# Down projection of a two-layer hybrid encoder: tiles 3 to 18 as four block groups of four in one chain instead of eight, four plain and four

## The chip, the cores and the metric

The kernel runs on one core of one Trainium2 chip. The metric is device time in microseconds, the median of several executions of the program. All arithmetic is float32; a matmul is done in three passes over float32r high and low parts, so that one product of float32 matrices is three matmul instructions.

## What is computed

Two layers over 1040 frames (16 learned meta tokens and 1024 input frames) of width 1024. Each layer has an attention half (a gated-linear-attention head group beside a forgetting-attention head group, one output projection, residual add) and a gated feed-forward half. Only the last matrix product of the second half is touched here:

```
def conv_ffn(x, w_up, conv_w, conv_b, w_down):
    h = x @ w_up
    ...
    u, g = jnp.split(hc, 2, axis=-1)
    return (jax.nn.silu(g) * u) @ w_down

# in each layer
h = h + conv_ffn(rms_norm(h, ffn_norm[i]), w_up[i], conv_w[i], conv_b[i], w_down[i])
```

`w_down` is 2816 x 1024. The kernel holds it as 22 tiles of 128 rows (the gated tiles, numbered 0 to 21) by 8 column blocks of 128.

## The kernel before

Activations are kept transposed: 128 features on the partitions, frames along the row. The frames are worked on in two halves of 520 in layer 0 (0 to 519 and 520 to 1039) and, since the last layer drops the meta tokens, in two halves of 512 in layer 1. A half of 520 is two matmuls of 260 columns ("pieces"), a half of 512 is one matmul.

**The gated tiles.** The up-projection writes each of the 22 gated tiles `cv` to memory (`actd`, L1395). For the down projection they are read back as `st` (L1458, L1464) and split into high and low float32r parts, the high part by a cast on ScalarE (ACT), the low part by a subtraction on VectorE (DVE). `prepare` (L1447) does this. It is a generator: `pump` lets it go on by a step when enough buffers are free, and `complete` runs it until what is needed now exists.

**The groups.** `GROUPS` (L49) says how the sum over the tiles is cut:

- "n", tiles 0 to 2, plain: for each of 8 column blocks and each half the three tiles are multiplied; ACT copies the sum out of PSUM to `do`, and a DMA issued by GpSimd (POOL) adds it to the residual in memory (`hm`, L1688).
- "s", tiles 3 to 10, a block group: see below; the sums are added to `hm` by DMA (L1588).
- "r", tiles 11 to 14, plain: the residual is read from memory to `h` (L1659) ahead of it, and DVE adds the products out of PSUM onto it (L1684).
- "s", tiles 15 to 18, a block group; the residual is on chip now, so DVE adds the sums `du` and `dg` onto `h` (L1585).
- `LAST`, tiles 19 to 21, plain, follows in `down_last` beside the next stage's norm.

**A block group** (`down_blocks`, L1555) is one level of a Strassen-Winograd product. Two column blocks (a "pair" j, 4 pairs in all) by two halves of the group's tiles are a 2 x 2 block matrix of weights, and two halves of the tiles by two halves of the frames are a 2 x 2 block matrix of activations. Seven products p = 1 to 7 take the place of eight. Per group, seven activation operands `X[p]` are formed once, with four combinations on DVE (L1517) and seven splits (L368 on ACT, L369 on DVE). Per pair, seven weight operands are formed: up to four combinations on DVE (L1114), and for each a cast on ACT (`hi`, L1132) and a subtraction on DVE (`lo`, L1133). With eight tiles a weight operand is 128 x 512, with four it is 128 x 256, and a product is 24 or 12 matmuls in layer 0 (12 or 6 in layer 1). The order of the products is written out in `seq`; it lets the next pair's first product begin before the pair's last two. Out of PSUM, ACT copies (L1594) and DVE adds (L1593).

**What sets the order.** PE's instructions stand in the order of the program text. Those of the other engines are put in order by a scheduler, from when it expects each to be ready, except where the text pins one (`keep_in_program_order`). Each engine, and SyncE (SP) with the DMA loads it issues, then works strictly in its order. The weight operands are written `AHEAD` = 4 products ahead of the product that uses them, and a buffer that is being added to memory by DMA counts as free `LANDING` = 4 products later.

Of the kernel before, what the change touches and what calls it, by code (L numbers as in the profile page):

```python
# [23 lines left out]
T = META + SEQ  # L24
# [143 lines left out]
class Kern:  # L168
# [1278 lines left out]
    def prepare(self, halves, acts, X):  # L1447
# [37 lines left out]
        for kind, g0, ng in GROUPS + (("r",) + LAST,):  # L1485
            while len(ahead) < 2 and loads:
                yield size()
                fetch()
# [16 lines left out]
            for k0 in range(0, nk, 2):  # L1505
                m = min(2, nk - k0)

                def put(p, src):
# [4 lines left out]
                    self.split(h, l, src[:, :m, :W])  # L1513
                    X[g0][p].append(([hi, lo] if m == 2 else [hi], h, l))

                def tt(out, a, b, op):
                    nc.vector.tensor_tensor(out=out[:, :m, :W], in0=a[:, :m, :W], in1=b[:, :m, :W], op=op)  # L1517
                yield m
# [36 lines left out]
    def down_blocks(self, lyr, g0, ng, X, pp, fw, halves, after, hT):  # L1555
# [3 lines left out]
        nk, o0, W = ng // 2, halves[0], halves[2]  # L1559
# [8 lines left out]
        j, k = NP - 2, NP - 1  # L1568
        seq += [(j, 2), (j, 6), (j, 5), (k, 1), (j, 7), (k, 6), (j, 4), (j, 3), (k, 7), (k, 2), (k, 5), (k, 4), (k, 3)]
        raws, ops, st = {}, [], {}  # L1570
        wd = lambda m: self.wd[lyr, m][:, g0:g0 + ng, :]

        def ensure(i):
            while len(ops) < min(i + 1, len(seq)):
                j, p = seq[len(ops)]
                ops.append(self.block_operand(wd(2 * j), wd(2 * j + 1), nk, j, p, fw, raws, len(ops) % 2))
                if nk == 2 and p == 6 and j + 1 < NP:
                    self.block_raws(wd(2 * j + 2), wd(2 * j + 3), nk, j + 1, fw, raws)
# [3 lines left out]
        def hand_on(i, m, x):  # L1582
            if hT:
# [7 lines left out]
        def evacuate(i, j, p):  # L1591
# [17 lines left out]
            elif p == 4:  # L1609
                copy(q["g"][:, t0])  # L1610
                hand_on(i, 2 * j + 1, q["g"])
            elif p == 3:
                add(q["u"][:, t1], q["x"])
                hand_on(i, 2 * j, q["u"])
                del st[j]
        def run():
            self.among_blocks = True
            for i, (j, p) in enumerate(seq):
                ensure(i + AHEAD)
# [6 lines left out]
                ops[i] = None  # L1626
                for k in range(nk):
                    _, hi, lo = X[p][k // 2]
# [4 lines left out]
                while going and (going[0][0] <= i or i == len(seq) - 1):  # L1633
# [12 lines left out]
    def ffn_down(self, lyr, pp, fw, halves, acts, X, ids):  # L1646
# [9 lines left out]
        def load_residual():  # L1656
            for k in range(KD):
# [260 lines left out]
```

## Time and profile before

| | |
|---|---|
| time, median of 3 runs | 2490.31 us (2489.84 to 2492.92) |
| the profiled execution | 2491.14 us, of it the span of its instructions 2489.4 |
| granted TensorE clock, mean | 0.997 |
| TensorE busy | 2455.0 us, 18286 matmuls |
| VectorE busy | 1884.3 us |
| ScalarE busy | 1331.6 us |
| GpSimd busy | 386.7 us |
| DMA moved | 261.02 MB, mean 105 GB/s |
| down projection, layer 0: first plain matmul, first and last block product | 1007.4, 1041.8 and 1207 us |
| down projection, layer 1: first block product, last copy of one | 2279 and 2439 us |

In the profile, PE is TensorE's matmuls and PEld its weight loads, DVE is VectorE, ACT is ScalarE, POOL is GpSimd, and SP issues DMAs. A row names a line of the kernel, an engine, an operation and "out<-in" by the program's tile names. "idle before" is how long the engine stood idle just ahead of such rows, and behind the arrow is what ended it.

### The profile page before, as it was taken

What the parts mean: (1) busy time and instruction counts of PE and PEld (TensorE: products, weight loads), DVE (VectorE), ACT (ScalarE), POOL (GpSimd) and SP (SyncE); (2) the same over time, 40 slices, a digit from 0 to 9 for tenths busy, and PEclk for the clock granted to TensorE, in tenths of its full rate; (3) what the DMA queues carried; (4) which work ended last, traced back from release to release, by engine and by line L of the source; (5) the groups of instructions that cost most, each with busy time, mean ns of one, the idle gap of its engine ahead of it and who ended that gap; (6) DMA issues with size and microseconds to landing.
All of it is one profiled execution on the core that took longest, in us unless ns stands there. A gap on an engine that the chain in (4) does not pass through costs nothing.

```text
span 2489.4 us, 47411 instructions
## 1 busy us (share of the span) xinstructions
PE 2455.0 (99%) x18286; PEld 2361.6 (95%) x18286; DVE 1884.3 (76%) x3833; ACT 1331.6 (53%) x2889; POOL 386.7 (16%) x567
## 2 busy tenths in 40 slices
PE   9999999999999999999999999999999999999998
PEld 8999999999999999999999899999999999997886
DVE  8656776869988888865865666777699888887567
ACT  7346666636555555642543466666465555555433
POOL 2023333210000000100210334331100000001002
PEclk9999999999999999999999999999999999999999
DMA  3232134433322224763312222243433212247722
GB/s 134 67 90 68 47 97 125 129 119 111 108 82 81 88 67 143 196 171 120 111 52 77 75 76 73 70 142 108 146 81 115 90 64 90 76 160 178 211 69 87
DMA packets 122002, 261.02 MB, mean 105 GB/s; under 512 B 15264, under 2 KB 37024, under 8 KB 121776
## 3 DMA queue, kind: packets, MB, share of 16 engines
q1 hardware_dynamic: 97440, 182.81, 23.8%
q0 software_dynamic: 22464, 72.88, 10.3%
q8 instruction: 143, 2.34, 0.4%
q10 hardware_dynamic: 1872, 2.31, 0.3%
q14 instruction: 83, 0.68, 0.1%
HBM read 177.31 MB, written 67.85 MB: 98 GB/s over the span
## 4 chain that ended last, share of the span: by engine, by line
PE 67%; issue 16%; DVE 11%; ACT 4%; DMA 1%; POOL 0%; SPq 0%; DVEq 0%; POOLq 0%; ACTq 0%
PE mm L254 7%; PE mm L256 7%; PE mm L255 7%; PE up L254 5%; PE up L255 5%; PE up L256 5%; PE down L255 5%; PE down L256 5%; PE down L254 5%; PE av L752 3%; PE tr L726 2%; DVE S L693 1%; PE S L690 1%; PE wo L254 1%; PE wo L256 1%
## 5 line engine op out<-in xcount | busy, mean ns | idle before, releaser
L254 PE MATMUL up<-x,hi 128*128 128x260 f32 x2240 | 632.8, 283 | 0.1
L255 PE MATMUL up<-x,lo 128*128 128x260 f32 x2240 | 632.8, 283 | 0.0
L256 PE MATMUL up<-x,hi 128*128 128x260 f32 x2240 | 632.7, 282 | 0.1
L256 PEld LDWEIGHTS up<-x,hi 128*128 128x128 f32 x2240 | 422.0, 188 | 0.4 <-DVE x L1157 0.3
L254 PEld LDWEIGHTS up<-x,hi 128*128 128x128 f32 x2240 | 421.6, 188 | 0.5 <-DVE hg L1370 0.3
L255 PEld LDWEIGHTS up<-x,lo 128*128 128x128 f32 x2240 | 421.4, 188 | 0.1
L1132 ACT CAST hi<-raw 128x512 fp32r<-128x512 f32 (+1 forms) x490 | 265.5, 553 | 197.4 <-PE up L256 88.1
L254 PE MATMUL mm<-xh,hi 128*128 128x348 f32 (+4 forms) x1056 | 362.8, 344 | 0.0
L1133 DVE TENSOR_TENSOR lo<-raw,hi 128x512 fp32r<-128x512 f32 (+1 forms) x490 | 287.1, 600 | 84.1 <-ACT hi L1132 83.8
L256 PE MATMUL mm<-xl,hi 128*128 128x348 f32 (+4 forms) x1056 | 339.9, 322 | 0.0
L255 PE MATMUL mm<-xh,lo 128*128 128x348 f32 (+4 forms) x1056 | 339.4, 321 | 0.0
L254 PEld LDWEIGHTS mm<-xh,hi 128*128 128x128 f32 x1056 | 199.6, 189 | 5.2 <-issue 4.6
L255 PEld LDWEIGHTS mm<-xh,lo 128*128 128x128 f32 x1056 | 199.5, 189 | 0.7 <-issue 0.7
L256 PEld LDWEIGHTS mm<-xl,hi 128*128 128x128 f32 x1056 | 198.5, 188 | 0.4 <-issue 0.3
L1114 DVE TENSOR_TENSOR raw<-raw,raw 128x512 f32<-128x512 f32 (+1 forms) x230 | 147.2, 648 | 24.2 <-DMA raw<-in_wd_dram 21.9
L705 ACT ACTIVATE P<-S,m 116x460 f32<-116x460 f32 (+2 forms) x224 | 125.0, 562 | 71.0 <-DVE m L693 67.3
L255 PE MATMUL down<-x,lo 128*128 128x260 f32 (+1 forms) x504 | 161.2, 320 | 0.8 <-DVE lo L1133 0.8
L254 PE MATMUL down<-x,hi 128*128 128x260 f32 (+1 forms) x504 | 161.0, 319 | 0.0
L256 PE MATMUL down<-x,hi 128*128 128x260 f32 (+1 forms) x504 | 161.0, 319 | 0.0
L369 DVE TENSOR_TENSOR PT<-tr,PT 116x464 fp32r<-116x464 f32 (+3 forms) x240 | 122.9, 515 | 47.4 <-ACT PT L368 45.7
L221 ACT CAST hi<-raw 128x512 fp32r<-128x512 f32 (+2 forms) x152 | 87.3, 575 | 111.3 <-PE wo L256 37.5
L1395 POOL DMA_DIRECT2D actd<-cv x44 | 23.6, 537 | 745.5 <-DVE cv L1394 727.3
(310 smaller groups left out, 5996.1 us busy)
## 6 DMA issues: line engine op xcount, KB each, us to landing
raw<-in_wm_dram SPq DMA_DIRECT2D x330, 256.0 KB, 3.0
raw<-in_wd_dram SPq DMA_DIRECT2D x48, 256.0 KB, 4.6
actd<-cv POOLq DMA_DIRECT2D x22, 520.0 KB, 3.0
actd<-cv POOLq DMA_DIRECT2D x22, 512.0 KB, 3.1
cb<-cd SPq DMA_DIRECT2D x16, 520.0 KB, 4.0
hm<-h POOLq DMA_DIRECT2D x32, 260.0 KB, 2.8
kA<-kA SPq DMA_DIRECT2D x24, 260.0 KB, 4.0
kL<-kL SPq DMA_DIRECT2D x24, 260.0 KB, 4.5
```

Source lines behind the costliest of these rows:

```text
L221: nc.scalar.copy(hi[:, :n, :], raw[:, :n, :])
L254: nc.tensor.matmul(ps, wh, xh[:, c0:c0 + n], start=first, stop=False, skip_group_check=more)
L255: nc.tensor.matmul(ps, wl, xh[:, c0:c0 + n], start=False, stop=False, skip_group_check=more)
L256: nc.tensor.matmul(ps, wh, xl[:, c0:c0 + n], start=False, stop=last, skip_group_check=more)
L369: nc.vector.tensor_tensor(out=lo, in0=src, in1=hi.bitcast(F32), op=ALU.subtract)
L690: nc.tensor.matmul(S[:rows, :n], q["qA"][e][:, qs], q["kA"][e][:, c0:k1], start=True, stop=False)
L705: nc.scalar.activation(P[:rows, :n], S[:rows, :n], AF.Exp, scale=-1.0, bias=m[:rows, nch - 1:nch], accum_out=(den if nch == 1 else d3[:row ...
L726: nc.tensor.transpose(tr[:w, 3 - j, :rows], P[:rows, o:o + w], id_)
L752: nc.tensor.matmul(av[:, a:b], w.rearrange("p a b -> p (a b)"), x, start=(t == ts[0] and part == 0 and i == 0), stop=(t == last and i == 1))
L1114: nc.vector.tensor_tensor(out=q[out][:, :nk, :], in0=q[a][:, :nk, :], in1=q[b][:, :nk, :], op=op)
L1132: nc.scalar.copy(hi[:, :nk, :], src[:, :nk, :])
L1133: nc.vector.tensor_tensor(out=lo[:, :nk, :], in0=src[:, :nk, :], in1=hi[:, :nk, :].bitcast(F32), op=ALU.subtract)
```

## The change

`GROUPS` becomes five groups: "n" as before, and then four block groups of four tiles, 3 to 6, 7 to 10, 11 to 14 and 15 to 18. There is no "r" group left. The four run as one chain: `down_blocks` gets all of them, the pairs are numbered 0 to 15, and `seq` runs on from the last pair of a group to the first of the next as it does from pair to pair. The first three groups add to `hm` by DMA; the residual is read in the last group, six blocks after product 6 of its first pair and two after product 6 of its second, and the last group's sums are added on chip. The activation operands of a group are formed while the group ahead is multiplied; their casts and low parts are pinned to the program order there, and so are the residual's loads. `LANDING` is 8.

```
-GROUPS, LAST = (("n", 0, 3), ("s", 3, 8), ("r", 11, 4), ("s", 15, 4)), (19, 3)
+GROUPS, LAST = (("n", 0, 3), ("s", 3, 4), ("s", 7, 4), ("s", 11, 4), ("s", 15, 4)), (19, 3)
-LANDING = 4
+LANDING = 8
...
@@ prepare
-            while len(ahead) < 2 and loads:
+            while len(ahead) < (1 if kind == "s" and self.among_blocks else 2) and loads:
...
-                    self.split(h, l, src[:, :m, :W])
+                    hi_ = nc.scalar.copy(h, src[:, :m, :W])
+                    lo_ = nc.vector.tensor_tensor(out=l, in0=src[:, :m, :W], in1=h.bitcast(F32), op=ALU.subtract)
+                    if self.among_blocks:
+                        self.tc.keep_in_program_order(hi_)
+                        self.tc.keep_in_program_order(lo_)
...
+                for _ in range(2 if self.among_blocks else 0):
+                    yield 0
@@ down_blocks
-        NP = KD // 2
+        NP, N = KD // 2, KD // 2 * len(groups)
...
-        for j in range(1, NP - 2):
+        for j in range(1, N - 2):
             seq += [(j, 2), (j, 6), (j, 5), (j, 7), (j + 1, 1), (j, 4), (j, 3)]
...
-                if nk == 2 and p == 6 and j + 1 < NP:
-                    self.block_raws(wd(2 * j + 2), wd(2 * j + 3), nk, j + 1, fw, raws)
+                if p == 6 and j + 1 < N:
+                    self.block_raws(*wd(j + 1), nk, j + 1, fw, raws)
...
-            if hT:
+            m = 2 * (j % NP) + half
+            if j >= N - NP:
...
+                if p == 1 and j % NP == 0:
+                    complete(lambda: built(groups[j // NP]))
                 ensure(i + AHEAD)
...
-                if j == NP - 1:
-                    for held, _, _ in X.pop(p):
+                if j % NP == NP - 1:
+                    for held, _, _ in X[g0].pop(p):
                         s.put(*held)
-                    if len(ops) == len(seq):
-                        after()
-                    self.pump(1, 3)
-                elif j and p == 5:
+                if (j, p) == (N - NP, 6):
+                    load_residual(range(6))
+                if (j, p) == (N - NP + 1, 6):
+                    load_residual(range(6, KD))
+                if i % 2 and (j >= N - NP or not built(groups[j // NP + 1])):
                     self.pump(1, 4)
@@ ffn_down
-        def load_residual():
-            for k in range(KD):
+        def load_residual(which):
+            for k in which:
                 hT.append(s.get(F32, f"h{k}", first=ids))
-                nc.sync.dma_start(hT[k][:, o0:T], self.hm[k][:, o0:T])
+                self.tc.keep_in_program_order(nc.sync.dma_start(hT[k][:, o0:T], self.hm[k][:, o0:T]))
```

What moves on the engines, at two places. The first is VectorE in layer 0. Before, this is a piece of its queue in the only group of four, tiles 15 to 18, that carries the residual: `lo` are low parts of weight operands, `du` and `dg` sums of a pair, `h1` and `h0` the residual, `al` the low part of a tile of `LAST`.

```order
L1593 TENSOR_TENSOR dg_15286<-down_15257,dg_15286 128x520
L1133 TENSOR_TENSOR lo_15320<-raw2_15289,hi_15319 128x256
L1593 TENSOR_TENSOR du_15214<-down_15305,du_15214 128x520
L1133 TENSOR_TENSOR lo_15339<-raw2_15070,hi_15338 128x256
L1585 TENSOR_TENSOR h1_14685<-dg_15286,h1_14685 128x1040
L1593 TENSOR_TENSOR du_15214<-down_15257,du_15214 128x520
L1133 TENSOR_TENSOR lo_15357<-raw_15297,hi_15356 128x256
L1585 TENSOR_TENSOR h0_14683<-du_15214,h0_14683 128x1040
L1593 TENSOR_TENSOR du_15233<-down_15360,du_15233 128x520
L1133 TENSOR_TENSOR lo_15375<-raw2_15072,hi_15374 128x256
L1133 TENSOR_TENSOR lo_15393<-raw_15074,hi_15392 128x256
L1496 TENSOR_TENSOR al_15412<-st_14541,ah_15411 128x1040
```

Of the change, this is a piece of VectorE's queue in the second group, tiles 7 to 10, at its second pair. L1521 and L1514 are the lines that were L1517 and L369, L1603 was L1593; `x6`, `x5` and `x7` belong to the third group.

```order
L1521 TENSOR_TENSOR st_13408<-st_13417,t2_14523 128x1040
L1514 TENSOR_TENSOR x6_14526<-t2_14523,x6_14525 128x1040
L1133 TENSOR_TENSOR lo_14548<-raw_14425,hi_14547 128x256
L1133 TENSOR_TENSOR lo_14576<-raw2_14573,hi_14575 128x256
L1603 TENSOR_TENSOR dg_14563<-down_14534,dg_14563 128x520
L1521 TENSOR_TENSOR st_13414<-st_13414,t2_14523 128x1040
L1514 TENSOR_TENSOR x5_14568<-st_13408,x5_14567 128x1040
L1133 TENSOR_TENSOR lo_14603<-raw2_14571,hi_14602 128x256
L1133 TENSOR_TENSOR lo_14626<-raw2_14421,hi_14625 128x256
L1603 TENSOR_TENSOR du_14440<-down_14534,du_14440 128x520
L1514 TENSOR_TENSOR x7_14621<-st_13411,x7_14620 128x1040
```

In the place of residual additions and low parts of `LAST`, operations over a full row in both, stand combinations and low parts of the next group's activations, between the low parts of weights and the additions out of PSUM that are as wide as before.

The second place is SP's queue where the residual is read, layer 0. Before, the loads of `h` stand with weights of the plain group "r" (L212) and with tiles of `LAST` (L1458), ahead of most weights of the group 15 to 18 (L1099):

```order
L1659 DMA h5_14693<-hm5_106 128x1040
L1659 DMA h0_14683<-hm0_101 128x1040
L1458 DMA st_14822<-actd20_129 128x1040
L212 DMA raw_14882<-in_wd_dram 128x512
L1659 DMA h7_14697<-hm7_108 128x1040
L212 DMA raw_14940<-in_wd_dram 128x512
L1458 DMA st_15409<-actd21_130 128x1040
L1659 DMA h6_14695<-hm6_107 128x1040
L212 DMA raw_14998<-in_wd_dram 128x512
L1099 DMA raw_15056<-in_wd_dram 128x256
```

Of the change (L1674 was L1659), with the weights of the last group's first three pairs:

```order
L1674 DMA h0_15574<-hm0_101 128x1040
L1099 DMA raw2_15335<-in_wd_dram 128x256
L1099 DMA raw2_15337<-in_wd_dram 128x256
L1099 DMA raw_15477<-in_wd_dram 128x256
L1674 DMA h1_15576<-hm1_102 128x1040
L1458 DMA st_15604<-actd20_129 128x1040
L1458 DMA st_15656<-actd21_130 128x1040
L1099 DMA raw2_15479<-in_wd_dram 128x256
L1099 DMA raw2_15481<-in_wd_dram 128x256
L1099 DMA raw_15483<-in_wd_dram 128x256
L1674 DMA h2_15578<-hm2_103 128x1040
L1674 DMA h3_15580<-hm3_104 128x1040
```

The residual's loads moved in among the weight loads of the chain: `raw2_15335` and `raw2_15337` belong to the last group's first pair and now stand behind `h0`, and the weights of its second pair stand behind `h1` and two tiles of `LAST`.

More of the change, by code (lines that the diff above doesn't have):

```diff
@@ L1626, in run @@
                 ops[i] = None
+                g0 = groups[j // NP][0]
                 for k in range(nk):
-                    _, hi, lo = X[p][k // 2]
+                    _, hi, lo = X[g0][p][k // 2]
                     for c in range(pieces):
@@ L1670, in plain @@
                 complete(lambda: all(j in acts for j in range(g0, g0 + ng)))
-                if kind == "r" and not hT:
-                    load_residual()
             if kind == "n" and m == 0:
@@ L1693, in plain @@
                     s.put(*acts.pop(j))
-            if not (nxt and built(nxt)):
+            if not (nxt and built(nxt[0])):
                 self.pump(2)
@@ L1700, in ffn_down @@
             if kind == "s":
-                parts.append((g0, ng))
+                if not isinstance(parts[-1], tuple):
+                    parts.append(())
+                parts[-1] += ((g0, ng),)
                 continue
@@ L1717, in run @@
                 if not isinstance(part, list):
-                    complete(lambda: built(part))
                     blocks[1]()
@@ L1721, in run @@
                 if nxt:
-                    then = parts[i + 2] if i + 2 < len(parts) else []
-                    blocks = self.down_blocks(lyr, *nxt, X[nxt[0]], pp, fw, halves,
-                                              lambda t=then: t and len(ahead) < 2 and fetch(t), hT)
+                    blocks = self.down_blocks(lyr, nxt, X, pp, fw, halves, hT, load_residual, complete, built)
                 for k, t in enumerate(part):
@@ L1732, in run @@
                 ahead.clear()
-            if not hT:
-                load_residual()
             complete(lambda: all(j in acts for j in range(LAST[0], sum(LAST))))
```

20 lines of the change are left out of this document (11 added, 9 removed).

## Prediction

> **What bounds the kernel now.** I read the page's table of engines first, then stages of the down projection, then the waits inside them.
>
> ```profile
> PE 2455.0 (99%) x18286; PEld 2361.6 (95%) x18286; DVE 1884.3 (76%) x3833; ACT 1331.6 (53%) x2889; POOL 386.7 (16%) x567
> ```
>
> TensorE (PE) is busy in 99% of the span. Since matmuls overlap, I do not lean on that share but on how many start in a stretch. The next rows are two stretches inside the down projection, one for each layer, all of it between the first block product and the last: length, then busy us and (count) of PE, PEld, DVE, ACT and POOL, the granted clock, the DMA share and GB/s.
>
> ```profile
> 1042.00:1202.00 160.00, 160.00 (x1337) 160.00 (x1337) 94.59 (x148) 61.30 (x109) 7.66 (x9) 1.00 0.51 141
> 2282.00:2438.00 156.00, 156.00 (x675) 126.48 (x674) 96.00 (x151) 59.65 (x107) 6.83 (x8) 1.00 0.50 140
> ```
>
> A matmul of 260 columns takes 160/1337 = 0.1197 us in layer 0, and one of 512 columns 156/675 = 0.2311 us in layer 1, at a granted clock of 1.00 and with no idle PE. So this part ends when PE ends, and its length is the number of matmuls. Only the run-up in layer 1 has holes:
>
> ```profile
> 2250.00:2260.00 10.00, 9.91 (x43) 7.78 (x42) 10.00 (x11) 9.02 (x14) 2.70 (x4) 1.00 0.55 105
> 2260.00:2270.00 10.00, 9.81 (x43) 7.64 (x42) 7.94 (x9) 6.17 (x9) 1.31 (x2) 1.00 0.93 222
> 2270.00:2280.00 10.00, 9.18 (x40) 7.19 (x39) 10.00 (x13) 8.91 (x16) 3.19 (x4) 1.00 1.05 194
> ```
> ```profile
> PE down L255 <- DVE lo L1133: 0.8, 1, 0.8
> PE down L254 <- ACT do L1686: 0.2, 1, 0.2
> ```
>
> PE loses 0.09 + 0.19 + 0.82 = 1.1 us there. The second fence (who waited for whom between 2240 and 2290: us, times, longest) puts 0.8 us of it on the first weight operand of the block group, which VectorE (DVE) forms behind the activation operands of eight tiles.
>
> **The change, part by part.** *Matmuls.* The two groups of four out of tiles 3 to 10 multiply as often as the group of eight did: 4 pairs x 7 products x 2 x 2 x 2 x 3 = 672 in layer 0. Tiles 11 to 14 were plain, 8 x 2 x 4 x 2 x 3 = 384; as a block group they need 4 x 7 x 2 x 2 x 3 = 336. That is 48 fewer in layer 0, and, with one piece for two, 24 fewer in layer 1: 48 x 0.1197 + 24 x 0.2311 = 5.74 + 5.55 = **11.3 us less on PE**, on the path.
>
> [...]
>
> *DVE.* What it needs per block group of four: 28 subtractions for the low parts of weights, 16 combinations of weights (both 256 wide), 12 additions out of PSUM, and 11 operations over a full row (four combinations and seven low parts of the next group's activations; in the last group eight residual additions and three low parts). Rows by shape (count | busy us, mean ns), layer 0 and then layer 1:
>
> ```profile
> L1133 DVE TENSOR_TENSOR lo<-raw,hi 128x256 fp32r<-128x256 f32 x28 | 11.0, 417 | 2.4 <-ACT hi L1132 2.4
> L1593 DVE TENSOR_TENSOR du<-down,du 128x520 f32<-128x520 f32 x15 | 10.4, 692 | 3.6 <-PE down L256 3.6
> ...
> L369 DVE TENSOR_TENSOR x<-st,x 128x1040 fp32r<-128x1040 f32 x6 | 7.3, 1235 | 3.9 <-DMA hm<-du 3.9
> L1114 DVE TENSOR_TENSOR raw<-raw,raw 128x256 f32<-128x256 f32 x16 | 6.3, 420 | 1.9 <-DMA raw<-in_wd_dram 1.8
> ```
> ```profile
> L1593 DVE TENSOR_TENSOR du<-down,du 128x512 f32<-128x512 f32 x16 | 11.0, 684 | 4.3 <-PE down L256 4.3
> L1496 DVE TENSOR_TENSOR al<-st,ah 128x1024 fp32r<-128x1024 f32 x7 | 8.5, 1221 | 4.1 <-ACT ah L1495 4.1
> ```
>
> By durations a group costs 28 x 0.417 + 16 x 0.420 + 12 x 0.692 + 11 x 1.235 = 40.3 us in layer 0, and 40.1 in layer 1. PE needs 336 x 0.1197 = 40.2 and 168 x 0.2311 = 38.8. That would be too much, but rows in a queue that is not waiting start before the one ahead has ended. This is DVE in the last group of layer 0 (start, duration or span of xN):
>
> ```profile
> 1182.64 0.69 DVE L1593 TENSOR_TENSOR du<-down,du 128x520 f32<-128x520 f32 x1
> 1183.25 0.75 DVE L1133 TENSOR_TENSOR lo<-raw,hi 128x256 fp32r<-128x256 f32 x2
> 1183.92 1.23 DVE L1496 TENSOR_TENSOR al<-st,ah 128x1040 fp32r<-128x1040 f32 x1
> 1185.07 0.75 DVE L1133 TENSOR_TENSOR lo<-raw,hi 128x256 fp32r<-128x256 f32 x2
> 1185.74 1.09 DVE L1114 TENSOR_TENSOR raw<-raw,raw 128x256 f32<-128x256 f32 x3
> 1186.75 0.69 DVE L1593 TENSOR_TENSOR dg<-down,dg 128x520 f32<-128x520 f32 x1
> ```
>
> From start to start an addition takes 0.61 us, a 256-wide row 0.335, a full row 1.15. So a group takes 44 x 0.335 + 12 x 0.61 + 11 x 1.15 = 34.7 us: 86% of PE's time in layer 0 and 89% in layer 1. The nearest stage is the last group of before, which has the same 28, 16, 12 and 11, though some of them are done ahead of it:
>
> ```profile
> 1168.00:1208.00 40.00, 40.00 (x336) 40.00 (x335) 30.66 (x55) 21.55 (x46) 0.00 (x0) 1.00 0.17 47
> 2400.00:2440.00 40.00, 40.00 (x174) 32.39 (x173) 30.87 (x56) 22.07 (x48) 0.00 (x0) 1.00 0.16 47
> ```
>
> DVE is busy for 31 of 40 us and PE has no hole. Four such groups in a row, each some 4 us fuller, still leave DVE 4.1 to 5.5 us of slack per group. I cost DVE's extra rows at nothing; PE's 40 us hide them. At full durations, with no cover, they cost 4 x 0.1 + 4 x 1.3 = 5.6 us.
>
> *ACT* casts and copies, and one row of POOL that is used below:
>
> ```profile
> L1132 ACT CAST hi<-raw 128x256 fp32r<-128x256 f32 x28 | 11.2, 409 | 24.1 <-PE down L256 20.7 <-DMA raw<-in_wd_dram 2.8 <-ACT hi L1132 0.6
> L1594 ACT COPY du<-down 128x520 f32<-128x520 f32 x16 | 9.5, 593 | 17.1 <-PE down L256 14.3 <-DMA hm<-do 2.7
> ...
> L368 ACT CAST x<-st 128x1040 fp32r<-128x1040 f32 x6 | 6.4, 1063 | 10.7 <-DMA hm<-dg 6.5 <-DVE st L1517 2.7 <-DVE al L1496 1.5
> ```
> ```profile
> L1588 POOL DMA_DIRECT2D hm<-du x4 | 3.4, 847 | 8.9 <-DVE du L1593 5.4 <-DVE raw L1114 3.4
> ```
>
> 28 x 0.409 + 16 x 0.593 + 7 x 1.063 = 28.4 of 40 us, hidden. Landing 8 instead of 4 keeps the same time, 8 x 1.44 = 11.5 us against 4 x 2.87: a product is now 12 matmuls, 1.44 us, and was 24. The new pins hold casts and low parts of activations in the written order, so that one that waits for its load has copies out of PSUM (ACT) or additions (DVE) behind it, and PE waits for those; the loads are issued a group ahead, so I cost the pins at nothing.
>
> *DMA.* Two more groups add into memory, 16 transfers of 520 KB per layer. Queues in layer 0 between 1041 and 1120 us (packets, MB, share of 16 engines):
>
> ```profile
> q1 hardware_dynamic: 4488, 9.36, 35.1%
> q0 software_dynamic: 1282, 4.73, 34.8%
> ...
> hm<-du POOLq DMA_DIRECT2D x3, 520.0 KB, 7.0
> ```
>
> 4.73 MB are 8.9 such transfers in 0.348 x 79 = 27.5 us, 3.1 each, so 16 cost 50 us of the engines. The part had a share of 0.51 over 160 us, 82 us; it becomes 132 in 154, 0.85. That fits, and an addition lands in 7.0 us, inside the 11.5. Their issue is 16 more rows on POOL of 0.85 us, 14 us in a queue that the first stretch shows busy for 8 of 160. The residual's eight loads, on SP's queue, now stand among the weights of the last group instead of ahead of plain tiles; the lead of one pair (7 x 1.44 = 10 us) covers them. I cost DMA at nothing, with this bound: the longest waits of DVE for weights in the two parts were these (the idle time before the row, and what ended it, in brackets):
>
> ```profile
> 1055.93 1.42 DVE L1114 TENSOR_TENSOR raw<-raw,raw 128x512 f32<-128x512 f32 x2 [9.07 <-DMA raw<-in_wd_dram]
> ```
> ```profile
> 2292.37 1.42 DVE L1114 TENSOR_TENSOR raw<-raw,raw 128x512 f32<-128x512 f32 x2 [8.43 <-DMA raw<-in_wd_dram]
> ```
>
> 9.1 and 8.4 us, both ended some 13 us into the group of eight. They cost PE nothing, because four operands formed ahead were 11.5 us of work. Four operands are now 5.7 us in layer 0 and 5.5 in layer 1, so such a wait would cost 3.4 + 2.9 = 6.3 us.
>
> *Run-up.* Half of the activation operands that DVE formed before the first block product are now due 40 us later, so the 0.8 us hole in layer 1 should close (between 0 and 1.1). *New small waits:* between nothing and the rivals below; the nearest row is what PE waited in this part of before, 0.8 + 0.2, so I take 1.0.
>
> **Sum:** -11.3 - 0.8 + 1.0 = -11.1 us. From the profiled execution, 2491.14 us (span 2489.4 and 1.7 around it), that gives 2480.0; it ran 0.8 us above the median of 2490.31, so I predict **2479.2**.
>
> **Rivals.** *DVE becomes the bound.* If rows cost their full durations, PE waits 5.6 us: 2484.8. For it: 86 to 89% leaves little when DVE also waits for casts. Against it: the start-to-start rows above.
>
> [...]
>
> *Weights late at the head of the chain.* The 9.1 and 8.4 us waits come again, with half the cover: 2479.2 + 6.3 = 2485.5. For it: the additions of the plain group crowd the DMA engines there as before. Against it: a pair's weights are half as many bytes.
>
> *Slower.* With a DMA share of 0.85 the same wait comes at the head of every group, where the next group's activations, or the residual, go through SP ahead of weights while additions are in flight: four times per layer, 4 x 6.3 = 25 us, 2504. It decides from the fourth wait on (12 us), and beyond 0.2% slower from the sixth.
>
> *No gain.* If a group's activations are not formed in time, PE stands at three borders per layer, and a third of the 13 us of forming each set would eat the gain: about 2490.
>
> **How the numbers follow.** Forecast 0.55, DVE bound 0.13, late weights 0.17, slower 0.10, no gain 0.05. A measurement of this kernel can tell about 0.2%, 5 us, from no change, so the line lies at 2485.3. Faster: 0.55, most of the DVE case (0.10) and half of the late weights (0.09), 0.74; slower 0.10; the rest 0.16. The range runs from all gains without new waits (2490.31 - 11.3 - 1.1 = 2477.9, a little under it) to 1.5 above the third case: 2477.5 to 2487, which holds 0.85.
>
> **What would show it.** Right: 72 fewer matmuls, down-projection stretches with PE at its full count up to the last block product, each about 5.6 us shorter; DVE near 9 tenths there with gaps that PE does not share; the hole at 2275 gone. Wrong: PE rows "down" that wait for low parts of weights (DVE bound, if DVE is then without idle; late weights, if DVE itself waits for raw), for activations, or SP waiting on additions into memory ahead of weight loads.

## The result, and the profile after

The changed kernel takes 2528.05 us, median of 4 runs (2522.28 to 2532.76), against 2490.08 (2489.84 to 2492.92) before: a ratio of 1.0143, 95% interval 1.0131 to 1.0155. It is 38 us slower where 11 us faster was forecast. The profiled execution took 2526.35 us, its span is 2524.6 and its mean granted clock 0.990 (0.997 before).

The row of engines from the page, and the two stretches inside the chain, one for each layer (length, then PE, PEld, DVE, ACT, POOL, granted clock, DMA share, GB/s):

```profile
PE 2459.2 (97%) x18214; PEld 2360.2 (93%) x18214; DVE 1936.4 (77%) x4023; ACT 1387.9 (55%) x3055; POOL 415.2 (16%) x599
```
```profile
1040.00:1200.00 160.00, 144.71 (x1159) 143.46 (x1160) 113.77 (x219) 87.23 (x177) 23.87 (x28) 0.95 0.80 183
2280.00:2440.00 160.00, 147.22 (x598) 115.87 (x597) 113.77 (x220) 84.31 (x174) 24.67 (x29) 0.95 0.82 187
```

The 72 matmuls are gone. But at the rates of before, 1159 matmuls need 138.7 us and 598 need 138.2: 43 of these 320 us are lost. PE stands idle for 15.3 + 12.8 = 28 of them; most of the other 15 are the clock, 0.95 where it was 1.00. Who waits for whom on PE, from the plain group to the end of the chain (us, times, longest), first layer 0, then layer 1:

```profile
PE down L254 <- DVE dg L1603: 10.4, 4, 5.6
PE down L254 <- DVE du L1603: 4.7, 2, 3.5
PE down L254 <- ACT do L1699: 3.3, 1, 3.3
```
```profile
PE down L254 <- DVE dg L1603: 7.3, 5, 3.6
PE down L254 <- DVE du L1603: 4.2, 2, 3.1
PE down L254 <- ACT do L1699: 2.3, 1, 2.3
```

15 waits, 32.2 us: 13 of them, 26.6 us, for an addition out of PSUM on DVE (`dg`, `du`, L1603), two, 5.6 us, for a copy out of PSUM on ACT (`do`). The span grew by 35.2 us although 11.3 us of matmuls left it, so 46.5 went. 32.2 are the idle time. The trace's record of the granted clock has the rest: in the two chains the clock falls to 0.50 seven times, for 34 us together, and PE works in 28 of these, which costs it 14.0 us. Why was the addition late? The longest wait, 5.6 us, begins at 1057.03 and ends at 1062.64. DVE ahead of it (start, duration, in brackets the idle time before and what ended it):

```profile
1049.37 0.42 DVE L1133 TENSOR_TENSOR lo<-raw,hi 128x256 fp32r<-128x256 f32 x1 [0.95 <-ACT hi L1132]
1056.96 0.88 DVE L1114 TENSOR_TENSOR raw<-raw,raw 128x256 f32<-128x256 f32 x2 [7.17 <-DMA raw<-in_wd_dram]
1057.77 1.23 DVE L1514 TENSOR_TENSOR x<-st,x 128x1040 fp32r<-128x1040 f32 x1
1058.92 0.42 DVE L1133 TENSOR_TENSOR lo<-raw,hi 128x256 fp32r<-128x256 f32 x1
1059.25 1.24 DVE L1521 TENSOR_TENSOR st<-st,t 128x1040 f32<-128x1040 f32 x1
1060.41 1.23 DVE L1514 TENSOR_TENSOR x<-st,x 128x1040 fp32r<-128x1040 f32 x1
1061.56 0.42 DVE L1133 TENSOR_TENSOR lo<-raw,hi 128x256 fp32r<-128x256 f32 x1
1061.89 0.69 DVE L1603 TENSOR_TENSOR dg<-down,dg 128x520 f32<-128x520 f32 x1
```

DVE stood 7.17 us at a combination of weights whose load had not landed. The addition that PE waited for is behind it in DVE's queue. PE's wait begins only after the load has landed: DVE then has two combinations, two low parts and three rows of 1040 columns for the next group's activations to do, 4.9 us, before it comes to the addition. So the rows of the change lengthen a wait that a late load began. In layer 0 DVE lost 27.1 us in 7 such waits, in layer 1 30.8 in 10:

```profile
DVE raw L1114 <- DMA raw<-in_wd_dram: 27.1, 7, 7.2
```
```profile
DVE raw L1114 <- DMA raw<-in_wd_dram: 30.8, 10, 6.9
```

ACT is held up in the same way: ahead of the copies of `do` that PE waits for until 1040.23 it stands at the cast of a late weight.

```profile
1038.26 1.02 ACT L1132 CAST hi<-raw 128x256 fp32r<-128x256 f32 x3 [7.46 <-DMA raw<-in_wd_dram]
```

And SP, which issues those loads in order (L1099), itself stood 112 us of layer 0's chain until weight buffers had been read. Before, it stood 66 us there, so waiting for buffers is not new by itself. After:

```profile
SPq L1099 <- DVE lo L1133: 68.7, 28, 10.5
SPq L1099 <- DVE raw L1114: 43.1, 17, 11.6
```

### The profile page after: what moved, and what is told of

The parts are those of the page before. It is cut to its first block, busy times and chain, and to the rows that moved or that the text cites. A ratio compares the mean times of both kernels' runs of the same rounds, so it can differ in the third digit from the quotient of the medians.

```text
span 2524.6 us, 47927 instructions
## 1 busy us (share of the span) xinstructions
PE 2459.2 (97%) x18214; PEld 2360.2 (93%) x18214; DVE 1936.4 (77%) x4023; ACT 1387.9 (55%) x3055; POOL 415.2 (16%) x599
## 5 line engine op out<-in xcount | busy, mean ns | idle before, releaser
L1132 ACT CAST hi<-raw 128x256 fp32r<-128x256 f32 (+1 forms) x602 | 296.8, 506 | 209.9 <-PE up L256 88.1
L1133 DVE TENSOR_TENSOR lo<-raw,hi 128x256 fp32r<-128x256 f32 (+1 forms) x602 | 317.5, 543 | 83.8 <-ACT hi L1132 82.9
L254 PE MATMUL down<-x,hi 128*128 128x260 f32 (+1 forms) x672 | 221.5, 330 | 26.7 <-DVE dg L1603 17.7
L255 PE MATMUL down<-x,lo 128*128 128x260 f32 (+1 forms) x672 | 219.5, 327 | 0.0
L256 PE MATMUL down<-x,hi 128*128 128x260 f32 (+1 forms) x672 | 219.1, 326 | 0.0
L1114 DVE TENSOR_TENSOR raw<-raw,raw 128x512 f32<-128x512 f32 (+1 forms) x294 | 165.0, 571 | 61.9 <-DMA raw<-in_wd_dram 59.2
L254 PEld LDWEIGHTS down<-x,hi 128*128 128x128 f32 x672 | 130.5, 194 | 42.2 <-DVE dg L1603 21.0
L369 DVE TENSOR_TENSOR PT<-tr,PT 116x464 fp32r<-116x464 f32 (+3 forms) x240 | 123.0, 515 | 47.3 <-ACT PT L368 45.7
```

Of the source, the lines that this page charges most:

```text
L254: nc.tensor.matmul(ps, wh, xh[:, c0:c0 + n], start=first, stop=False, skip_group_check=more)
L255: nc.tensor.matmul(ps, wl, xh[:, c0:c0 + n], start=False, stop=False, skip_group_check=more)
L256: nc.tensor.matmul(ps, wh, xl[:, c0:c0 + n], start=False, stop=last, skip_group_check=more)
L369: nc.vector.tensor_tensor(out=lo, in0=src, in1=hi.bitcast(F32), op=ALU.subtract)
L1114: nc.vector.tensor_tensor(out=q[out][:, :nk, :], in0=q[a][:, :nk, :], in1=q[b][:, :nk, :], op=op)
L1132: nc.scalar.copy(hi[:, :nk, :], src[:, :nk, :])
```

## The experiments

The theory after this: weights land too late, DVE waits for them with additions out of PSUM behind it, PE waits for the PSUM buffer (`down`) that they read, and the granted clock falls behind each wait. The rivals: DVE or ACT has too much to do; DMA engines full of additions into memory; the residual's burst. "After" below is the changed kernel. The kernel before was run again beside each round of runs, so a ratio is not exactly the quotient with 2490.08.

| run | us, median | ratio to before | 95% interval |
|---|---|---|---|
| e1_packed | 2508.57 | 1.0069 | 1.0054 to 1.0084 |
| e2_packed_lead2 | 2501.72 | 1.0044 | 1.0028 to 1.0061 |
| e3_no_adds | 2501.19 | 1.0037 | 1.0025 to 1.0048 |
| e4_spread | 2525.14 | 1.0129 | 1.0106 to 1.0151 |
| e5_ahead5 | 2532.75 | 1.0154 | 1.0137 to 1.0171 |
| e6_lead2_spread | 2501.25 | 1.0034 | 1.0023 to 1.0046 |
| e7_lead2_spread_head | 2509.97 | 1.0068 | 1.0053 to 1.0083 |
| e8_before_stall | 2511.68 | 1.0077 | 1.0062 to 1.0092 |
| e9_paced | 2505.85 | 1.0063 | 1.0046 to 1.0079 |
| e10_paced_only | 2535.32 | 1.0175 | 1.0160 to 1.0190 |
| e11_split_only | 2523.80 | 1.0127 | 1.0106 to 1.0147 |
| e12_no_pins | 2581.86 | 1.0365 | 1.0349 to 1.0380 |
| e13_no_weight_loads | 2480.80 | 0.9957 | 0.9942 to 0.9972 |
| e14_act_queue | 2523.05 | 1.0120 | 1.0100 to 1.0141 |
| e15_act_queue_late | 2511.01 | 1.0082 | 1.0059 to 1.0105 |
| e16_pieces | 2500.34 | 1.0040 | 1.0026 to 1.0054 |
| e17_spread_forming | 2511.97 | 1.0085 | 1.0071 to 1.0099 |
| e18_lead3_late | 2486.64 | 0.9981 | 0.9972 to 0.9990 |

### Are late weights the whole cause?

After, with the chain's weights filled in place of loaded:

```
# block_raws, nk == 2
-    nc.sync.dma_start(q[name][:, :nk, :], src[:, k0:k0 + nk, :])
+    nc.gpsimd.memset(q[name][:, :nk, :], 0.01)
```

> The kernel after with the chain's weights not loaded: GpSimd fills their buffers with 0.01 (so the four groups multiply by constants), everything else is the same, the same casts, low parts, combinations, additions into memory, activation and residual loads, pins. Theory: late weights are the whole cause; with weights always there PE has no wait over 1 us in the chains and the forecast of the prediction comes true, 2477 to 2483. If DVE or ACT is too full, or activations or residual come late, waits of PE stay without weights too: over 2487.

2480.80 us: the forecast, to 1.6 us. Two stretches inside the chain of this kernel:

```profile
1050.00:1200.00 150.00, 150.00 (x1255) 150.00 (x1255) 128.17 (x242) 93.06 (x192) 36.40 (x77) 1.00 0.70 150
2290.00:2440.00 150.00, 149.89 (x645) 120.64 (x645) 129.66 (x246) 90.16 (x188) 35.02 (x74) 1.00 0.67 146
```

PE has no hole beside a DVE that is busy for 128 and 130 of 150 us with all rows of the change. DVE and ACT are not the bound; one wait of 2.3 us is left in layer 0, for weights of the plain group, and one of 0.5 in layer 1. The run takes more away, though, than the lateness of weights: their load on the DMA engines too (share 0.70 where after has 0.80), and their place in SP's queue, so that activations and the residual go out earlier.

One part of the change alone, the group of eight as two groups of four:

```
-("s", 3, 4), ("s", 7, 4), ("s", 11, 4), ("s", 15, 4)
+("s", 3, 4), ("s", 7, 4), ("r", 11, 4), ("s", 15, 4)   # r: plain, residual read ahead of it
```

> One part of the change alone: tiles 3 to 10 as two block groups of four in one chain, tiles 11 to 14 plain as before, the last four a chain of their own, the residual loaded ahead of the plain tiles as before. No matmul is saved; there are 8 more additions into memory per layer. Theory of late weights (products of half the time, loads the same number of products ahead, that land as late as before): the stalls of the first two groups come as in the kernel after, 17.8 us of idle PE and half as much lost clock: 2508 to 2520. If the third group or the residual inside the chain is what makes the chain late: 2490 to 2496.

2523.80 us, by its ratio 32 us over before; 2508 to 2520 had been expected, and it lies above that. The split, which saves no matmul, brings the loss (1.0127 of 1.0143). The rest of the change saves all 72 matmuls, 11 us, and the total is no better for it, so it must lose at least as much again. In the split's profiled execution (2517.12 us, the fastest of four) PE waits 21.5 us in the plain group and the two groups of four behind it, none in the last group. The first row is layer 0's, the others are layer 1's:

```profile
PE down L254 <- DVE du L1603: 7.3, 1, 7.3
```
```profile
PE down L254 <- DVE dg L1603: 6.0, 3, 4.4
PE down L254 <- ACT dg L1604: 5.9, 1, 5.9
```

What did the split halve? Not the lead. In a group of eight, before, a pair's weights are asked for only with its first operand, four products of 2.87 us, 11.5 us, ahead of the combination that DVE waits at. The changed kernel asks for them three products earlier: the combination is seven products of 1.44 us, 10 us, behind. So "loads the same number of products ahead", as the expectation has it, is not how the text stands for a group of eight. What halved is the time that the weight buffers hold. They are the same buffers in both, for two pairs at most: 2 x 7 x 2.87 = 40 us of PE's work in a group of eight, 20 us in a group of four, where each is half empty. SP can't issue a load until a buffer has been read (the 112 us above), and what a load needs to land did not halve. Loads of weights inside the chain of layer 0 (KB each, median us from issue to landing), before and after:

```profile
raw<-in_wd_dram SPq DMA_DIRECT2D x15, 256.0 KB, 5.3
```
```profile
raw<-in_wd_dram SPq DMA_DIRECT2D x57, 128.0 KB, 5.9
```

### Do operands formed ahead cover a late weight?

```
-AHEAD = 4
+AHEAD = 5
```

> The kernel after with five operands formed ahead in place of four. If operands formed ahead are the cover against late weights, as the prediction had it, one more covers 1.44 us (1.39 in layer 1) of each of the 12 or so stalls of PE, and some 15 us of idle PE and 6 to 8 us of lost clock go: about 2505. If the additions out of PSUM that stand behind the waiting DVE instruction stop PE, and not a missing operand, the order on DVE shifts by one operand and nothing is gained: 2522 to 2534.

2532.75: nothing gained. An operand more in hand is no cover, because the wait holds the additions out of PSUM too, and PE stops where it needs their PSUM buffer: in the trace of this run as in after's, all of PE's waits in the chains (36 us) are for additions and copies out of PSUM, none for an operand (`hi`, `lo`).

### Buffers, lead and additions

In a group of four each weight buffer was half empty. Two matrices share one, and then the loads come a pair earlier as well:

```
# block_raws, nk == 2: one tile for A11 and A12, one for A21 and A22, one for S1 and S2
# e2, down_blocks, in place of "if p == 6 and j + 1 < N: self.block_raws(j + 1)"
+ if p == 6:
+     for a in (j + 1, j + 2): ... self.block_raws(*wd(a), nk, a, fw, raws)
```

> In the block groups the two weight halves of a matrix share one buffer, and the two sums S1 and S2 share one, so the same memory holds 4 and 3.5 pairs of weights where it held 2 and 1.75; each load is still issued at the same product of the pair ahead. If the weight loads stand on the queue because their buffers are not free (SP waits 112 us for readers of weight buffers in the chain of layer 0), most of the 32 us of idle PE go and the time falls to about 2490. If the loads are simply issued too few products before their use, or the DMA engines are too full, or DVE has too much to do, the time stays at 2520 to 2530.

> The same shared buffers, and the weights of a pair are loaded one pair (7 products, 10 us) earlier. Theory of late weights (a lead of three products is 4.3 us where loads land in 5.4 to 7): idle PE in the two chains falls from 32 us to under 8, the granted clock stays near 1.00, and the time is 2480 to 2492. Rival, the DMA engines are too full with 16 more additions into memory per layer: the weights are late all the same, 2510 to 2525. Rival, DVE has too many rows: 2520 to 2530, with DVE busy where PE stands.

2508.57 and 2501.72: both fell between their two ranges. Some 20 us are back by buffers, 7 more by the lead, and 12 over before are left. In e2 PE waits in layer 0 are down to 7.3 us, in layer 1 to 10.7 in the same window, with one long wait in each last group (6.4 and 8.1).

```
# e3, hand_on
-    nc.gpsimd.dma_start(self.hm[m][:, o0:T], x[:, o0:T], accum_op=ALU.add)
+    if j // NP not in (1, 2): nc.gpsimd.dma_start(...)
```

> Leaves out the additions into memory of the second and third block group (16 transfers of 520 KB per layer), so that these two groups' share of the sum is missing and the chain moves no more of them than the group of eight did. Rival of the DMA load: the DMA share of the chain falls from about 0.8 to 0.5, the stalls go, 2480 to 2495. Theory of too short a lead: loads land sooner with emptier engines, but SP still issues them late; about half of the idle PE stays, 2500 to 2515. DVE theory: 2520 to 2530.

2501.19, in the second range. What is left stands at the head, in the plain and the first group, whose additions this run keeps. From the second group on PE hardly waits, with weights issued as late as in after (SP stands 110 us of layer 0's chain for buffers, in after 112), and even while the residual comes in at 329 GB/s:

```profile
1150.00:1160.00 10.00, 10.00 (x85) 10.00 (x85) 10.00 (x17) 7.88 (x14) 0.00 (x0) 1.00 0.00 0
1160.00:1170.00 10.00, 10.00 (x86) 10.00 (x85) 9.60 (x21) 5.94 (x13) 0.00 (x0) 1.00 0.98 329
```

So neither theory falls: with additions in flight loads land late (before's 128 KB loads of weights, issued after its last addition into memory of layer 0, landed in 2.1 us, those of after's chain in 5.9; DVE waited 8.5 us for weights in layer 0 of e3, 27.1 in after), and with few buffers and a short lead that matters. Additions left out, or buffers and lead given, each brings some 26 us back.

### Bursts of other loads

```
# e4, down_blocks: two row blocks of the residual after product 6 of each pair of the last group
# e6: e2, and these one pair earlier (the condition shown is e6's; e4 has j >= N - NP)
+ if p == 6 and N - NP - 1 <= j < N - 1: load_residual(two row blocks)
# e7: e6, and block_raws(0), block_raws(1) three column blocks earlier in the plain group
```

> The residual's eight row blocks are loaded two per pair during the last block group instead of six at once and two a pair later. Theory: the burst stands ahead of weights on SP's queue and fills the DMA engines (share 1.05 between 1170 and 1190 us), and causes only the last group's stalls, 6 us of idle PE in layer 0 and 4 in layer 1 with some 5 us of lost clock; without it 2510 to 2516. If the short lead alone makes the stalls: 2524 to 2530.

> The shared weight buffers, a pair more of lead, and the residual loaded two row blocks at a time, from the last pair of the third group on, so that no load stands in SP's queue for an addition that was issued shortly before. Theory (SP's queue, where residual loads wait 13.4 us for additions into memory with weights behind them): the stalls in the last group, 5.6 us in layer 0 and 8.1 in layer 1, and the clock lost behind them go; the head of the chain in layer 1 keeps its 3 us: 2483 to 2489. If the DMA engines at a share of 1.05 are the reason, the stalls stay: 2497 to 2503.

> As the kernel with the spread residual, and the weights of the chain's first two pairs are loaded three products of the plain group earlier. Theory of late weights: the stalls at the head go too, no PE wait over 1 us is left in the two chains: 2479 to 2484. If the head is late because of the additions and activation loads on the DMA engines: within 2 us of the kernel with the spread residual.

2525.14, 2501.25 and 2509.97: the first two in their second range, e7 missed. Spreading the residual gave 3 us at most, and in e6 the last group's waits stayed, 6.9 and 7.5 us. Its SP queue and DVE show why (layer 0; SP rows: start, span of xN issues):

```profile
1156.70 1.04 SPq L1468 DMA_DIRECT2D st<-actd  x2
1157.85 0.47 SPq L1684 DMA_DIRECT2D h<-hm  x1
1158.41 0.46 SPq L1468 DMA_DIRECT2D st<-actd  x1
1158.97 2.05 SPq L1101 DMA_DIRECT2D raw<-in_wd_dram  x4
```
```profile
1173.11 0.43 DVE L1124 TENSOR_TENSOR raw<-raw 128x256 f32<-128x256 f32 x1 [9.90 <-DMA raw<-in_wd_dram]
```

Three tiles of `LAST` (`st`, 520 KB each) and a block of the residual go out within 2.2 us, and DVE's wait for the weights issued behind them, from 1158.97 on, ends at 1173.11. In e7 the early weights took the buffers that the plain group's own weights come through, and PE waited 4.3 us for those. Taking the bursts apart, with and without the buffers and lead:

```
# e9: e6; e10: after with e6's residual; both:
- if i % 2 and (j >= N - NP or not built(next group)):
+ if i % 2 and (j >= N - 2 if j >= N - NP else not built(next group)):   # LAST's tiles late
- while len(ahead) < (1 if kind == "s" and self.among_blocks else 2)
+ while len(ahead) < (1 if kind == "s" else 2)                           # third set not in the plain group
```

> The shared buffers, the pair more of lead and the spread residual, and two bursts taken apart: the activations of the last three tiles are loaded in the last two pairs instead of at the start of the last group, and the third group's activations no longer during the plain group. Theory: what is left of the stalls (6.9 and 7.5 us in the last group, 2.1 at the head of layer 1) comes from weight loads that land 12 us late behind such bursts, which move 325 GB/s at a DMA share of 1.05; without them idle PE is under 4 us in the two chains and the time is 2480 to 2487. Rival, the engines are too full on the mean (0.8), whatever the order: 2495 to 2503.

> The kernel after with its own buffers and lead, only the residual spread and the two bursts taken apart. If bursts are the main cause, 2490 to 2500; if the weight buffers and the lead of three products are, most of the stalls stay: 2510 to 2522.

2505.85 and 2535.32, both missed. In e9 the long waits of the last group are gone, but the third set of activations, eight loads of 2.1 MB in all, now goes out inside the chain, and there PE lost 8.3 us in layer 0 and 7.5 in layer 1. The moved burst took its wait with it: 8.3 and 7.5 us here, 6.9 and 7.5 in e6. Without buffers and lead (e10) all of it is worth nothing, it is even some 8 us slower than after.

```
# e14: e6, loads of activations and residual
- nc.sync.dma_start(...)
+ nc.scalar.dma_start(...)
# e15: e14, and LAST's tiles on that queue, late as in e9
```

> Shared buffers, a pair more of lead, residual two row blocks at a time, and the loads of the block groups' activations and of the residual issued on ScalarE's queue, so that weights on SP's queue stand behind no burst. If the queue's order makes weights late: the waits of 7 to 8 us in the last group go, 2480 to 2488. If the engines are full during a burst, whichever queue it comes from: weights land late all the same, 2496 to 2504. A load that ScalarE must wait with would hold copies out of PSUM behind it: over 2504, with PE waiting for ACT.

> As the kernel with loads on ScalarE's queue, and the activations of the last three tiles are on that queue too and come in the last two pairs only. If bursts of the whole load matter, a further 2 to 6 us less than that kernel; else within 3 us of it.

2523.05 and 2511.01: e14 in its third range, in which PE waits for ACT; e15 missed, 12 us less where 2 to 6 were expected. On a queue of their own, the bursts still make weights late, and activations too (waits of DVE, layer 0, e14):

```profile
DVE raw L1124 <- DMA raw<-in_wd_dram: 13.9, 4, 5.9
...
DVE st L1531 <- DMA st<-actd: 7.5, 1, 7.5
```

In e14 the tiles of `LAST` still go through SP's queue. In e15 that queue carries only weights in the chains, and DVE still waits 10.1 us for them around layer 0's chain and 8.1 around layer 1's, up to 5.0 at a time. So the order on SP's queue is not the whole reason: weights that have it to themselves are late too. ScalarE's own waits did not help: in layer 1 of e14 PE waits 5.3 us for a copy of `do`.

```
# e16: e9, a set's eight loads two by two, a step of the preparation with 6 of 7 products
# e17: e16, a piece with each product, the seven forming steps two products apart
```

> As the kernel with bursts taken apart, and a group's activations are asked for in four pieces, two products apart, instead of eight loads at once. If the bulk of 2.1 MB is what makes weights wait, the 8.3 and 7.5 us waits at the third set go: 2484 to 2492. If the pieces run together in SP's queue because they wait for the same buffers to come free, nothing changes: 2500 to 2508.

> As the kernel with loads in pieces, one piece per product, and the seven steps that form a group's activations two products apart instead of one. Theory: the last waits of PE, 6.4 us in layer 0 and 7.4 in layer 1, are additions that stand behind two or three full rows on DVE (1.15 us each, where a product is 1.44 us); spread, they go, and the time is 2480 to 2488, faster than both kernels. If DVE is too full on the whole (rows of 34.7 us in 40), waits of the same sum come at other places: 2496 to 2503.

2500.34 and 2511.97. The first lies in its second range, but not by that range's mechanism; the second missed. In e16 weights are hardly late (2.7 us of DVE waits in layer 0, 4.8 in layer 1), but eleven waits of PE of up to 2.7 us, 13.8 us in all, are for additions on DVE; in layer 0 they stand behind activation rows that DVE forms close together. So DVE's rows, bunched, can cost PE time even where weights are hardly late. Spread (e17), loads come late again: DVE waits 7.1 and 10.5 us for activations, up to 4.8 and 8.9 for weights, and PE up to 8.1.

### What a wait costs beyond itself

```
# before, plain "r", m in (2, 5), h == 0
+ for _ in range(3): nc.gpsimd.tensor_copy(scr[:, 0:W], out[:, first half])
+ nc.tensor.matmul(pz[:, 0, :128], self.ones[:], scr[:, 0:128], start=True, stop=True)
```

> The kernel before with four made stalls of PE, two in each layer in the plain group of tiles 11 to 14: GpSimd copies a half row three times and a small matmul waits for it (the copies are read by nothing else). It prices the clock by itself. If an idle PE costs only its idle time, the time rises by the sum of the four waits (estimated at 4 to 6 us each, 16 to 24 us). If the granted clock falls behind each wait as in the kernel after, it rises by about half as much again, with PEclk below 1.00 in the stretch behind each.

2511.68, a rise of 0.77%, 19.2 us (15.5 to 22.9). The four waits are 7.2 us in layer 0 and 5.6 in layer 1:

```profile
PE down L1690 <- POOL scr L1688: 7.2, 2, 4.4
```
```profile
PE down L1690 <- POOL scr L1688: 5.6, 2, 2.8
```

So 12.8 us of idle PE cost 19, 1.6 us more per wait (0.7 to 2.5 by the interval). The slices of 10 us around the two in layer 1 show it as clock; in the profiled execution's record the clock falls to 0.50 at each of the four waits, twice for 6.8 us and twice for 3.4, and PE loses 9.1 us by it:

```profile
2380.00:2390.00 10.00, 7.14 (x24) 5.29 (x23) 3.83 (x8) 0.00 (x0) 1.84 (x3) 0.83 0.27 96
2390.00:2400.00 10.00, 10.00 (x45) 8.11 (x44) 5.08 (x9) 2.27 (x5) 0.00 (x0) 1.00 0.10 26
2400.00:2410.00 10.00, 7.13 (x25) 5.30 (x24) 3.12 (x7) 0.63 (x1) 1.85 (x3) 0.84 0.10 27
```

### The pins

```
-                    if self.among_blocks:
-                        self.tc.keep_in_program_order(hi_)
-                        self.tc.keep_in_program_order(lo_)
# and none on the residual's loads
```

> The kernel after without the pins on the casts and low parts of the block groups' activations and on the residual loads. If the pins hold copies and additions behind casts that wait for loads, 2505 to 2518. If they cost nothing, as the prediction had it: 2522 to 2534.

2581.86, 54 us over after: outside both ranges. The run leaves out both kinds of pins at once, those of the casts and low parts and those of the residual's loads. Unpinned casts of activations are drawn forward in ACT's queue, to where their buffers are still being added to memory (waits of ACT, layer 0), and the copies out of PSUM wait behind them; among after's waits of ACT there is none of L1513 for an addition.

```profile
ACT x L1513 <- DMA hm<-du: 16.0, 4, 5.5
ACT x L1513 <- DMA hm<-do: 11.0, 2, 7.2
```

### A version that beats both

```
# after with shared buffers, the residual as in e6, LAST's tiles late as in e9, and
+ if p == 6:
+     for a in range(j + 1, min(j + (4 if j else 3), N)): self.block_raws(*wd(a), nk, a, fw, raws)
```

> Shared buffers, weights of the chain loaded three pairs ahead (two in its first pair), the residual two row blocks at a time, the last three tiles' activations only in the last two pairs. Theory: the waits of 7 to 8 us in the last group go, as in the kernel with bursts taken apart, and the third set of activations stays where it was, so that no new ones come; some 5 us of idle PE and 3 of lost clock stay: 2483 to 2491, about level with the kernel before or a little faster. If bursts make loads late by more than any lead that the buffers allow, or activations stop DVE instead: 2495 to 2505.

2486.64, median of 11 runs, ratio 0.9981 (0.9972 to 0.9990): 4.7 us, 0.2%, faster than before and 41 us faster than after. PE's waits, layer 0 and layer 1:

```profile
PE down L254 <- DVE dg L1614: 2.2, 2, 1.7
PE down L254 <- DVE du L1614: 0.5, 1, 0.5
```
```profile
PE down L254 <- ACT do L1708: 2.3, 1, 2.3
PE down L254 <- DVE du L1614: 1.1, 1, 1.1
PE down L254 <- DVE dg L1614: 0.7, 1, 0.7
```

6.8 us are left, and the granted clock falls in neither chain. Whether the third pair of lead or the later tiles of `LAST` did more was not run apart.

## Why the prediction was wrong

**The step that failed** is the one on DMA: "I cost DMA at nothing", with its bound of 6.3 us at the head of the chain "because four operands formed ahead" were cover. Three things in it were wrong. The time a load has was read from the bytes ("a pair's weights are half as many bytes") and from the lead ("7 x 1.44 = 10 us"). The lead is there in the text, but a load can't go out until a buffer is free. The work that the buffers hold halved, from 40 to 20 us, and landing did not (5.9 us against 5.3). Of the loss, e1 gets back 20 us by buffers alone, e2 7 more by a longer lead. The cover was no cover (e5): not an operand was missing but an addition or copy out of PSUM, behind the waiting row. And the bound stopped at one place per layer, while 17 waits of DVE for weights came in the two chains, and two of ACT, and with them the 15 waits of PE above: 32.2 us idle and 14.0 by the clock where 6.3 was the bound. The bill is 49 us between the forecast and the result; with weights always there the forecast comes true (e13, 2480.80 against 2479.2). How the loss of the split divides between its fuller DMA engines and its buffers was not run apart.

**Point by point.** *Matmuls*: 72 fewer, as said; e13 is 10.7 us (7.0 to 14.4) under before, where 11.1 was the sum. *DVE at nothing*: right where nothing is late, e13 (DVE busy for 128 and 130 of 150 us, PE without a hole); behind a late load DVE's rows lengthen the wait, as the rows around 1060 show. *ACT at nothing*: right, e13. *Landing 8*: additions landed in 6.3 (`dg`) and 7.4 us (`du`) of 11.5; it was not run alone. *Pins at nothing*: no run shows the cost that was weighed there; without the pins the kernel is 54 us slower (e12), which the forecast did not have, and which of the two kinds does it is open. *DMA share*: 0.85 forecast, 0.80 and 0.82 measured; right, and it should have raised the doubt. *Run-up hole in layer 1*: gone, as these slices show. In its place the plain group waits 3.3 and 2.3 us for `do`, which the forecast had not seen:

```profile
2250.00:2260.00 10.00, 10.00 (x85) 10.00 (x85) 10.00 (x12) 4.83 (x7) 0.53 (x1) 1.00 0.75 244
2260.00:2270.00 10.00, 10.00 (x52) 8.44 (x51) 10.00 (x12) 9.65 (x12) 0.00 (x0) 1.00 0.64 201
2270.00:2280.00 10.00, 10.00 (x44) 8.06 (x44) 7.50 (x8) 5.79 (x11) 3.22 (x5) 1.00 0.91 201
```

**The rivals.** "Slower" named the mechanism and the place, weights late at the head of every group behind activations or the residual while additions are in flight. It got a chance of 0.10 and a price of 2504. What it lacked is the additions out of PSUM behind the waiting row, and the clock: 25 us were put down, 32 of idle time and 14 of clock came. The sign the forecast gave for telling rivals apart held: DVE itself waits for `raw`, so it is late weights and not a full DVE.

## What to carry to other kernels

Count the buffers of a prefetch in microseconds of work, not in units: here the unit was halved and the buffers stayed one per unit, so that the work they hold fell from 40 to 20 us, while a load landed in 5.9 us where it had taken 5.3. Operands formed ahead covered no late load in this chain, because copies and additions out of PSUM that PE needed stood behind the waiting instruction in the same queue: a fifth operand gained nothing (e5, 2532.75 us). And an idle TensorE can cost more than its idle time: 32.2 us cost 46.5 here and 12.8 us cost 19 in e8, while the 6.8 us of e18 brought no fall of the clock.

## What the runs showed of the hardware that was not expected

The granted clock fell behind waits of PE of under 3 us (2.2 in after, 2.8 in e8). Slices of 10 us show 0.83 or 0.84 after one, and 0.66 to 0.69 in some others, and then 1.00 again. Taken over the fall alone the granted clock is 0.50 (after, 2332.45 to 2335.86; e8, 2386.33 to 2389.75), so 0.83 is 3.4 us of it, 1.7 us lost, and 0.66 twice that; e8's 1.6 us per wait fits. The shortest wait with a fall in after, 2.2 us, ended at 2332.18. It does not follow each wait: none came after the 3.3 us that ended at 1040.23.

```profile
1030.00:1040.00 10.00, 6.94 (x59) 6.73 (x57) 1.93 (x4) 2.33 (x6) 0.00 (x0) 1.00 0.70 166
2330.00:2340.00 10.00, 7.83 (x28) 6.23 (x28) 7.10 (x14) 3.87 (x9) 1.71 (x2) 0.83 0.71 145
```

And two slices of e16 have nearly the same idle time of PE, 2.46 and 2.72 us, one at a clock of 0.83 and one at 1.00:

```profile
1120.00:1130.00 10.00, 7.54 (x51) 7.36 (x50) 8.63 (x19) 3.55 (x9) 0.85 (x1) 0.83 0.92 248
2350.00:2360.00 10.00, 7.28 (x32) 5.59 (x31) 10.00 (x17) 5.89 (x12) 1.71 (x2) 1.00 0.98 248
```

So waits of 2.2, 2.5 and 2.8 us were enough for a fall in after, e16 and e8, and 2.7 us in e16 and 3.3 in after went without one. What decides it was not shown.
